# Attention heads issued as steps between weight stages, and another way to transpose queries, in a four-layer decoder trunk

## The chip, the cores and the metric

The kernel runs on one core of one Trainium2 chip. The metric is the device time of one execution in microseconds. Before the change three runs gave 2584.72, 2582.40 and 2582.67 us: a median of 2582.67.

## What is computed

A trunk of four layers on 256 tokens of width 2048, in float32. Each layer normalizes its input and multiplies it by one input matrix. That gives the streams of a token mixer, four query heads for attention over a memory of 256 tokens, and a gate. The heads' outputs are multiplied by SiLU(gate), go through an output matrix and are added to the residual. The mixers are, in order, latent attention (layer 0), sparse attention with an indexer (layer 1), sliding-window attention with a learned sink for each head (layer 2), and latent attention again (layer 3). A last normalization follows.

The change concerns layers 1 and 2. Both have 32 query heads of 64 features, in four groups of eight that share a key and a value head, and both add a bias by relative position. Of the reference (layer 2; layer 1 has no sink, and masks what the indexer did not select):

```python
s = jnp.einsum('bqgjd,bkgd->bgjqk', qb, kb, preferred_element_type=jnp.float32) * scale + bias
s = jnp.where(valid, s, NEG_INF)
m = jnp.maximum(jnp.max(s, axis=-1, keepdims=True), sink)
e = jnp.exp(s - m)
p = e / (jnp.sum(e, axis=-1, keepdims=True) + jnp.exp(sink - m))
return jnp.einsum('bgjqk,bkgd->bqgjd', p.astype(vb.dtype), vb)
```

## The kernel before

**Matrix products.** TensorE's products of two float32 matrices are made of three: each operand is a high part (the value rounded to the float32r type) and a low part (what is left), and high by high, high by low and low by high are summed. Weights come from HBM in stages of 2 or 4 tiles of 128 rows (`stage`, L206), loaded by SyncE's queue into five buffers. `parts_of` (L234) cuts a tile into its parts: ScalarE rounds it (through `copy_act`, L60), VectorE subtracts (in `split`, L69). There are three buffers of each part. `rows_by` (L240) gives tokens by columns, with the matmuls of L265 to L267; `columns_by` (L270) gives features by tokens, with those of L285 and L289. Both add up in a pair of the four PSUM tiles called acc.

**Steps.** `steps` (L227) is a list of Python generators. At each stage `other_work` (L229) advances the first of them twice, so that its instructions come into the program between two stages' matmuls. In layer 1 the indexer's selection is such a generator; in layer 3 a split of weights for the end is one. A row product over 2048 features has 8 stages, a gate has 8 (two products of 4), an output projection has 8 (four column chunks of 2), and the memory part's two query products have 8 together.

**Layers.** A layer runs six parts in the order memory heads 0 and 1 (part 4), groups 0 to 3, memory heads 2 and 3 (part 5). For each part it issues the projection, then the attention, and then `w_out` (L1134), the output projection of the part *before*. That adds into the residual x at L1139.

**A group** (class Grouped). `project` (L913) makes the eight heads' queries with `rows_by`, transposes them and makes the gate (`gate`, L474). In layer 1 `four_heads` (L461) takes the unsplit rows, transposes 4 blocks for each half of the heads (L467) and splits while it copies out of PSUM (L60, L471). In layer 2 `stacked` (L795) splits the rows first (L60, L801), sets the high and the low part of a head beside each other and transposes 16 blocks in float32r (`transposed`, L449, matmuls at L456). Then GpSimd's queue loads the group's table of biases, bm (L930), 1 MB, into a tile with one buffer, so the load waits until the group before has read its own.

`attend` (L934) first empties `steps`, and then issues all eight heads. A head is two score products (L943, L946), a bias and a running maximum on VectorE (L520 to L522), exponentials on ScalarE (L527), sums and reciprocals, three transposes of the weights (L502), and another split (L60, L69). After each second head comes the product with the values for both (L972). Heads 0 to 3 and 4 to 7 fill one half of y each, by a product with the gate (L978) and a split.

**Order.** `TileContext` sorts each engine's instructions itself, by what it takes to be ready at which time. What stands earlier in the program goes first among what is ready. So the trace's order isn't the program's, and waits are added where buffers or data are shared.

**Memory heads.** `memory_project` (L551) loads stored keys and values through GpSimd's queue and makes queries and a gate; `memory_attend` (L569) has two heads, with L580 as their score matmul and L601 as that with the values.

Of the kernel before, what the change touches and what calls it, by code (L numbers as in the profile page):

```python
# [8 lines left out]
F32 = mybir.dt.float32  # L9
# [6 lines left out]
P = 128  # L16
S = 256
# [9 lines left out]
N_TAB = 384  # L27
# [4 lines left out]
def kernel(ctx: ExitStack, tc: tile.TileContext, a: dict, out: bass.AP,  # L32
                             kinds=(0, 1, 2, 0)):
    nc = tc.nc
# [3 lines left out]
    act = ctx.enter_context(tc.tile_pool(name="act", bufs=1))  # L38
# [14 lines left out]
    def f32(ap):  # L53
        return ap.bitcast(F32)

    def part_tile(dt=F32R):
        return wk.tile([P, 512], dt, name="hl", tag="hl", bufs=2)

    def copy_act(o, i, scale=1.0):
        inst = nc.scalar.activation(o, i, AF.Copy, scale=scale)  # L60
        if pinned:
            tc.keep_in_program_order(inst)
# [164 lines left out]
    steps = []  # L227

    def other_work():  # L229
        for _ in range(2):  # L230
            if steps and next(steps[0], None) is None:
                steps.pop(0)

    def parts_of(wr, c0, n):  # L234
        wh = wp.tile([P, 512], F32R, name="wh", tag="wh", bufs=3)
# [225 lines left out]
    def four_heads(dst, rows_):  # L461

        tp = misc("tr")
        for t in range(2):
            for p in range(2):
                c = (2 * p + t) * P
                nc.tensor.transpose(tp[:, c:c + P], rows_[t][:, p * P:(p + 1) * P], ident)  # L467
        for h, main, low in ((0, slice(0, 64), slice(64, P)), (1, slice(64, P), slice(0, 64))):
            feats = tp[main].rearrange("p (j c) -> p j c", j=2)
            copy_act(dst[main, h::2, :], feats)  # L470
            nc.vector.tensor_sub(dst[low, h::2, :], feats, f32(dst)[main, h::2, :])  # L471


    def gate(nm, w, c0):  # L474
        gT = act.tile([P, 4, S], F32, name="gT", tag="gT", bufs=2)
        for h in range(2):
            acc = columns_by(nm.at, 16, w, 0, (c0 + h * S, S), "g")
            for j in range(2):
                z = total(acc[j])
                hz = wk.tile([P, S], F32, name="hz", tag="z", bufs=3)  # L480
                nc.vector.tensor_mul(hz, z, nm.half)
                th = wk.tile([P, S], F32, name="th", tag="e", bufs=4)
                nc.scalar.activation(th, hz, AF.Tanh)
                nc.vector.scalar_tensor_tensor(gT[:, 2 * h + j, :], th, 1.0, hz, op0=OP.add, op1=OP.mult)
        return gT
# [261 lines left out]
    class Grouped:  # L747
# [165 lines left out]
        def project(self, g):  # L913
            nm = self.nm
            acc = rows_by(nm.at, 16, self.w, 0, (g * 512, 512), "q")
            q = [act.tile([P, 4, S], F32R, name="qS", tag="pq", bufs=PQ) for z in range(2)]
            if self.sparse:
                for z in range(2):
                    rows_ = part_tile(F32)
                    for t in range(2):  # L920
                        copy_act(rows_[:, t * S:(t + 1) * S], acc[t][:, z * S:(z + 1) * S],
                                 scale=nm.col("eighth", t))
                    four_heads(q[z], [rows_[:, t * S:(t + 1) * S] for t in range(2)])
            else:
                for t in range(2):
                    self.stacked(lambda i0, i1: q[i0 // 4][:, :, t * P:(t + 1) * P], acc[t],
                                 nm.col("eighth", t), 8)
            bm = act.tile([P, 8, S], F32, name="bm", tag="big3")
            tab = tabs[0 if self.sparse else 1][g]
            nc.gpsimd.dma_start(bm, bass.AP(tensor=tab.tensor, offset=tab.offset + 127,  # L930
                                            ap=[[8 * N_TAB - 1, P], [N_TAB, 8], [1, S]]))
            return g, q, bm, gate(nm, self.w, self.g0 + g * 512)

        def attend(self, g, q, bm, gT):  # L934
            while steps:
                other_work()
            y = act.tile([P, 2, 4, S], F32R, name="y", tag="y", bufs=2)
            for h in (0, 2, 1, 3, 4, 6, 5, 7):
                def score(b):
                    sp = misc("sp")  # L940
                    qb = q[h // 4][:, h % 4, b * P:(b + 1) * P]
                    if b == 0:
                        nc.tensor.matmul(sp[:, :S], qb, self.k[:, g, :, :P], start=True, stop=True)  # L943
                    else:
                        for v in range(2):
                            nc.tensor.matmul(sp[:, :S], qb, self.k[:, g, v, :],  # L946
                                             start=v == 0, stop=v == 1)
                    return sp

                def bias(b, n):  # L950
                    bh = bm[:, h, S - n:]
                    if not self.sparse:
                        return bh
                    bs = wk.tile([P, S], F32, name="bs", tag="e", bufs=4)
                    nc.vector.tensor_add(bs[:, :n], bh, self.sel[:, b, :n])
                    return bs[:, :n]
                nsk = None if self.sparse else nsink[:, g * 8 + h:g * 8 + h + 1]
                tp = masked_softmax(score, bias, None, nsk)

                half, odd = h // 2 % 2, h % 2  # L960
                if half == 0:
                    pHL = [wk.tile([P, 3, 2, P], F32R, name="pT2", tag="pT", bufs=PT) for z in range(2)]
                split(pHL[0][:, :, half, :], pHL[1][:, :, half, :],
                      tp[:, :3 * P].rearrange("p (i c) -> p i c", i=3))
                if half == 0:
                    continue
                if not odd:
                    o = misc("o")
                v0 = g * P + (0 if odd else 64)
                for t in range(2):  # L970
                    for n_, (z, p_) in enumerate(((0, 0), (0, 1), (1, 0))):
                        nc.tensor.matmul(o[:, t * S:], self.vz[z][:, t, v0:v0 + P],  # L972
                                         pHL[p_][:, 2 * t:2 + t].rearrange("p i h c -> p (i h c)"),
                                         start=odd == t == n_ == 0, stop=odd == t == 1 and n_ == 2)
                if odd:
                    j = (h // 4) * 2
                    yt = tmp("yt")
                    nc.vector.tensor_mul(yt.rearrange("p (j b c) -> p j b c", j=2, b=2),  # L978
                                         o.rearrange("p (b j c) -> p j b c", b=2, j=2),
                                         gT[:, j:j + 2, :].rearrange("p j (b c) -> p j b c", b=2))  # L980
                    split(y[:, 0, j:j + 2, :], y[:, 1, j:j + 2, :], yt.rearrange("p (a b) -> p a b", a=2))
            return y


    def last_out(w, part, y):
# [140 lines left out]
    for i in range(depth):  # L1126
        kind = kinds[i]
        mixer = Latent(nm, i, kinds[:i].count(0)) if kind == 0 else Grouped(nm, i, kind == 1)
        mixer.first()
        if i == depth - 1:  # L1130
            steps.append(split_ahead(a["w_out"][i], 5))
        nxt = Norm(i + 1) if i + 1 < depth else None

        def w_out(part, y, last):  # L1134
            for c in range(4):
                acc = rows_by([y], 4, a["w_out"][i], part * 4, (c * 512, 512), "wo")
                for t in range(2):
                    xs = x[t][:, c * 512:(c + 1) * 512]
                    nc.vector.tensor_add(xs, xs, acc[t])  # L1139
                if c == 0 and copies:  # L1140

                    not_before(xs[:, :1])
                    table_copies(*copies.pop(0))
                if last and nxt is not None:
                    nxt.chunk(c)

        pending = None
        order = [4, 0, 1, 2, 3, 5]
        for n_, part in enumerate(order):
            if part >= 4:  # L1150
                y = memory_attend(*memory_project(nm, i, mixer.w, mixer.mq0, mixer.g0, part - 4,
                                                  f32(mixer.k[:, 0] if kind else mixer.kr)[:, 0, :1]))
            else:
                y = mixer.attend(*mixer.project(part))
            if pending is not None:
                w_out(*pending, False)
            pending = (part, y)
        if nxt is None:
            last_out(a["w_out"][i], *pending)
        else:  # L1160
            w_out(*pending, True)
            nxt.finish()
            nm = nxt
# [62 lines left out]
```

## Time and profile before

| | |
|---|---|
| median of three runs | 2582.67 us |
| the profiled execution, whole | 2583.45 us |
| its span, from the first to the last instruction | 2581.7 us |
| granted TensorE clock, mean | 0.999 |
| TensorE weight loads busy | 2210.8 us |
| VectorE, ScalarE busy | 1885.5, 1618.6 us |
| DMA | 520.02 MB, 201 GB/s in the mean |

Layer 1 runs from about 959 us of the span to 1492, layer 2 from there to about 1975. In the profile PE is TensorE's matmuls, PEld its weight loads, DVE VectorE, ACT ScalarE, POOL GpSimd, SP SyncE. L467 is line 467 of the kernel; a helper's line stands for all its callers, so the tiles' names (out<-in) tell which it was. In rows in order of time, the first number is the start in us from the span's beginning and the second the length. Matmuls overlap in their pipeline, so the time that one costs is the distance to the start of the next. "[0.34 <-DVE ms L583]" is idle time before an instruction, and what ended it. In rows of stretches each engine has its busy time and the number of its instructions, in the order PE, PEld, DVE, ACT, POOL, then the granted clock, the share of the DMA engines, and GB/s.

### The profile page before, as it was taken

The page shows a single profiled execution, that of the slowest core. Times are in us where ns is not written, and L with a number is a line of the kernel's source. Part 1 is how long each engine was busy: PE and PEld are TensorE (multiplying, and loading weights), DVE is VectorE, ACT ScalarE, POOL GpSimd, SP SyncE. Part 2 cuts the span into 40 slices and gives each one's busy share as a digit, 9 for nine tenths or more (in the row PEclk, how much of TensorE's full clock was granted, in tenths as well). Part 3 has the DMA queues.
Part 4 walks back from the last instruction along what each step waited for, and adds up shares of the span by engine and source line. Part 5 has one row for each costly group of instructions (what it writes and reads, how often), then busy time and mean ns, then how long its engine had stood idle before and what let it go on. Part 6 is the DMA issues. An engine that isn't in the chain of part 4 may idle for free. (4 is left out here: it accounts for less than half of the span.)

```text
span 2581.7 us, 41595 instructions
## 1 busy us (share of the span) xinstructions
PE 2569.7 (100%) x13986; PEld 2210.8 (86%) x13986; DVE 1885.5 (73%) x4139; ACT 1618.6 (63%) x3435; POOL 87.1 (3%) x159
## 2 busy tenths in 40 slices
PE   9999999999999999999999999999999999999998
PEld 7888898888888888888888888888888888888887
DVE  6666667677776686877778776777778767777676
ACT  6556556556656566667666666676666655665655
POOL 1000000000000010000000000000000000000000
PEclk9999999999999999999999999999999999999999
DMA  9888777666676667566556565555555877666664
GB/s 301 257 258 268 239 213 235 183 172 192 192 205 200 199 213 248 169 203 188 190 171 197 171 221 170 173 174 185 196 156 147 241 201 197 196 195 182 211 173 179
DMA packets 459416, 520.02 MB, mean 201 GB/s; under 512 B 69520, under 2 KB 353056, under 8 KB 457536
## 3 DMA queue, kind: packets, MB, share of 16 engines
q1 hardware_dynamic: 441744, 449.72, 58.1%
q0 software_dynamic: 16736, 66.65, 8.0%
q8 instruction: 110, 1.80, 0.3%
q14 instruction: 106, 0.87, 0.1%
q10 hardware_dynamic: 720, 0.98, 0.1%
HBM read 494.10 MB, written 35.75 MB: 205 GB/s over the span
## 5 line engine op out<-in xcount | busy, mean ns | idle before, releaser
L69 DVE TENSOR_TENSOR wl<-wr,wh 128x512 fp32r<-128x512 f32 (+2 forms) x1720 | 1159.9, 677 | 610.0 <-ACT wh L60 588.8
L60 ACT ACTIVATE wh<-wr 128x512 fp32r<-128x512 f32 (+2 forms) x1720 | 1065.3, 621 | 796.6 <-PE acc_g L285 176.9
L285 PE MATMUL acc_g<-xT,wh 128*128 128x512 f32 x1536 | 486.0, 396 | 0.0
L289 PEld LDWEIGHTS acc_g<-xT,wl 128*128 128x128 f32 x1536 | 284.6, 188 | 61.7
L289 PE MATMUL acc_g<-xT,wl 128*128 128x256 f32 x1536 | 307.9, 280 | 0.0
L266 PE MATMUL acc_wo<-wl,y 128*128 128x512 f32 x752 | 297.1, 395 | 0.2 <-DVE wl L69 0.2
L267 PE MATMUL acc_wo<-wh,y 128*128 128x512 f32 x752 | 292.0, 390 | 0.0
L285 PEld LDWEIGHTS acc_g<-xT,wh 128*128 128x128 f32 x1536 | 237.1, 189 | 2.7
L265 PE MATMUL acc_wo<-wh,y 128*128 128x512 f32 x752 | 234.5, 392 | 0.1
L266 PEld LDWEIGHTS acc_wo<-wl,y 128*128 128x128 f32 x752 | 141.3, 188 | 27.9 <-DVE wl L69 0.6
L267 PEld LDWEIGHTS acc_wo<-wh,y 128*128 128x128 f32 x752 | 141.3, 188 | 27.1
L265 PEld LDWEIGHTS acc_wo<-wh,y 128*128 128x128 f32 x752 | 139.1, 188 | 28.7 <-ACT y L60 1.0
L285 PE MATMUL acc_mq<-xT,wh 128*128 128x512 f32 x512 | 161.6, 396 | 0.0
L285 PE MATMUL acc_mk<-mT,wh 128*128 128x512 f32 x512 | 161.5, 396 | 0.1
L1139 DVE TENSOR_TENSOR x<-x,acc_wo 128x512 f32<-128x512 f32 x184 | 121.4, 681 | 3.7 <-PE acc_wo L267 3.6
L285 PE MATMUL acc_qn<-cT,wh 128*128 128x512 f32 x384 | 121.3, 397 | 0.0
L285 PE MATMUL acc_cq<-xT,wh 128*128 128x512 f32 x384 | 120.9, 396 | 0.0
L289 PEld LDWEIGHTS acc_mk<-mT,wl 128*128 128x128 f32 x512 | 96.1, 188 | 22.8 <-DVE wl L69 0.4
L289 PEld LDWEIGHTS acc_mq<-xT,wl 128*128 128x128 f32 x512 | 93.9, 188 | 20.1
L289 PE MATMUL acc_mq<-xT,wl 128*128 128x256 f32 x512 | 103.1, 281 | 0.0
L266 PE MATMUL acc_q<-wl,xT 128*128 128x512 f32 x256 | 101.2, 395 | 0.0
L289 PE MATMUL acc_mk<-mT,wl 128*128 128x256 f32 x512 | 101.1, 278 | 0.0
(328 smaller groups left out, 4326.2 us busy)
## 6 DMA issues: line engine op xcount, KB each, us to landing
wr<-in_w_out_dram SPq DMA_DIRECT2D x188, 512.0 KB, 3.7
wr<-in_w_in_a_dram SPq DMA_DIRECT2D x176, 512.0 KB, 4.5
wr<-in_w_mem_kv_dram SPq DMA_DIRECT2D x120, 512.0 KB, 4.6
wr<-in_w_in_b_dram SPq DMA_DIRECT2D x112, 512.0 KB, 3.4
wr<-in_w_in_c_dram SPq DMA_DIRECT2D x104, 512.0 KB, 3.5
wr<-in_w_uq_dram SPq DMA_DIRECT2D x192, 128.0 KB, 2.9
wr<-in_w_uq_dram SPq DMA_DIRECT2D x48, 256.0 KB, 3.8
tab<-flat POOLq DMA_DIRECT2D x8, 1536.0 KB, 9.7
```

The source lines that it names most:

```text
L60: inst = nc.scalar.activation(o, i, AF.Copy, scale=scale)
L69: nc.vector.tensor_sub(lo, src, f32(hi))
L265: nc.tensor.matmul(acc[t][:, :n], xh, wh[:, :n], start=first, stop=False)
L266: nc.tensor.matmul(acc[t][:, :n], xh, wl[:, :n], start=False, stop=False)
L267: nc.tensor.matmul(acc[t][:, :n], xl, wh[:, :n], start=False, stop=last)
L285: nc.tensor.matmul(acc[j], wh[:, o:o + P], q[:, :, kt % 4, :], start=kt == 0, stop=False)
L289: nc.tensor.matmul(acc[j][:, 0, :], wl[:, o:o + P], q[:, 0, kt % 4, :], start=False, stop=kt == kts - 1)
L1139: nc.vector.tensor_add(xs, xs, acc[t])
```

## The change

- `attend` of a group no longer issues its eight heads. It puts them as a generator (`heads`) into `steps`, in the order 0, 2, 1, 3, 4, 6, 5, 7, with 0, 6, 6, 5, 4, 4, 5 and 7 yields ahead of them. They come into the program between the stages of what follows: the output projection of the part before, the next queries, the next gate (or the memory part's products).
- Layer 2 transposes its queries as layer 1 does.
- The biases' tile is made once for a layer. Each group loads it in two halves, the first (heads 0 to 3) in `project`, the second in `attend`, after the steps are emptied.
- Ahead of the memory heads 2 and 3 of layers 1 and 2, `steps` is emptied.

```diff
+    def finish_steps():
+        while steps:
+            other_work()
...
             q = [act.tile([P, 4, S], F32R, name="qS", tag="pq", bufs=PQ) for z in range(2)]
-            if self.sparse:
-                for z in range(2):
-                    rows_ = part_tile(F32)
-                    for t in range(2):
-                        copy_act(rows_[:, t * S:(t + 1) * S], acc[t][:, z * S:(z + 1) * S],
-                                 scale=nm.col("eighth", t))
-                    four_heads(q[z], [rows_[:, t * S:(t + 1) * S] for t in range(2)])
-            else:
+            for z in range(2):
+                rows_ = part_tile(F32)
                 for t in range(2):
-                    self.stacked(lambda i0, i1: q[i0 // 4][:, :, t * P:(t + 1) * P], acc[t],
-                                 nm.col("eighth", t), 8)
-            bm = act.tile([P, 8, S], F32, name="bm", tag="big3")
+                    copy_act(rows_[:, t * S:(t + 1) * S], acc[t][:, z * S:(z + 1) * S],
+                             scale=nm.col("eighth", t))
+                four_heads(q[z], [rows_[:, t * S:(t + 1) * S] for t in range(2)])
+            if g == 0:
+                self.bm = act.tile([P, 8, S], F32, name="bm", tag="big3")
+            self.load_bias(g, 0)
+            return g, q, self.bm, gate(nm, self.w, self.g0 + g * 512)
+
+        def load_bias(self, g, half):
+
             tab = tabs[0 if self.sparse else 1][g]
-            nc.gpsimd.dma_start(bm, bass.AP(tensor=tab.tensor, offset=tab.offset + 127,
-                                            ap=[[8 * N_TAB - 1, P], [N_TAB, 8], [1, S]]))
-            return g, q, bm, gate(nm, self.w, self.g0 + g * 512)
+            nc.gpsimd.dma_start(self.bm[:, 4 * half:4 * half + 4, :],
+                                bass.AP(tensor=tab.tensor, offset=tab.offset + 127 + 4 * half * N_TAB,
+                                        ap=[[8 * N_TAB - 1, P], [N_TAB, 4], [1, S]]))
 
         def attend(self, g, q, bm, gT):
-            while steps:
-                other_work()
+
+            finish_steps()
+            self.load_bias(g, 1)
             y = act.tile([P, 2, 4, S], F32R, name="y", tag="y", bufs=2)
-            for h in (0, 2, 1, 3, 4, 6, 5, 7):
+            steps.append(self.heads(y, g, q, bm, gT))
+            return y
+
+        def heads(self, y, g, q, bm, gT):
+            for h, ahead in ((0, 0), (2, 6), (1, 6), (3, 5), (4, 4), (6, 4), (5, 5), (7, 7)):
+                for _ in range(ahead):
+                    yield True
                 def score(b):
...
             if part >= 4:
-                y = memory_attend(*memory_project(nm, i, mixer.w, mixer.mq0, mixer.g0, part - 4,
-                                                  f32(mixer.k[:, 0] if kind else mixer.kr)[:, 0, :1]))
+                projected = memory_project(nm, i, mixer.w, mixer.mq0, mixer.g0, part - 4,
+                                           f32(mixer.k[:, 0] if kind else mixer.kr)[:, 0, :1])
+                if kind and part == 5:
+                    finish_steps()
+                y = memory_attend(*projected)
```

More of the change, by code (lines that the diff above doesn't have):

```diff
@@ L981, in attend @@
                     split(y[:, 0, j:j + 2, :], y[:, 1, j:j + 2, :], yt.rearrange("p (a b) -> p a b", a=2))
-            return y
     def last_out(w, part, y):
```

## Prediction

> **What bounds the kernel now.** I read the page first, then busy time by stretches, then TensorE's instructions in order of time. From the page:
>
> ```profile
> span 2581.7 us, 41595 instructions
> ...
> PE 2569.7 (100%) x13986; PEld 2210.8 (86%) x13986; DVE 1885.5 (73%) x4139; ACT 1618.6 (63%) x3435; POOL 87.1 (3%) x159
> ...
> L69 DVE TENSOR_TENSOR wl<-wr,wh 128x512 fp32r<-128x512 f32 (+2 forms) x1720 | 1159.9, 677 | 610.0 <-ACT wh L60 588.8
> L60 ACT ACTIVATE wh<-wr 128x512 fp32r<-128x512 f32 (+2 forms) x1720 | 1065.3, 621 | 796.6 <-PE acc_g L285 176.9
> ```
>
> TensorE is busy for 2569.7 of 2581.7 us, so 12.0 us at most is plain idleness. The engines that cut each weight tile into two parts (L60, then L69) have room: ScalarE's largest wait before L60 is for matmuls. TensorE is what they wait for, not the other way round. One group of the layer with sinks (eight heads, the next queries, a gate, an output projection) looks like this in the view of stretches:
>
> ```profile
> 1717.40:1794.80 77.40, 77.40 (x409) 65.57 (x409) 59.32 (x149) 53.00 (x130) 0.89 (x1) 1.00 0.57 177
> ```
>
> In 77.4 us TensorE is never idle, while VectorE is free for 77.4 - 59.3 = 18.1 us and ScalarE for 24.4. The change touches just these stretches: four groups in layer 1 and four in layer 2. So only two things can shorten them: fewer cycles of TensorE's own, and the few places at which a matmul starts late.
>
> Are the heads in one lump now, because the code issues all eight ahead of the output projection? The row for the first score matmul of a head, over the window 1636 to 1700, says no:
>
> ```profile
> L943 PE MATMUL sp<-kd,qS x7: 280/363/364, 1639.1 to 1695.2; 128*128 128x256 f32 x7
> ```
>
> Seven starts lie over 56.1 us, one head every 9.4 us, in a period of 77.4. The order that is made out of the program has spread them already.
>
> **The change, term by term.**
>
> Term 1, the transposes of the queries in layer 2. Now a group splits its queries into high and low halves first, and transposes 16 blocks. TensorE's rows in order of time (start, length, instruction):
>
> ```profile
> 1689.97 0.88 PE L456 MATMUL tr<-identr,hl 128*128 128x128 f32 x8
> 1690.69 0.46 PE L266 MATMUL acc_wo<-wl,y 128*128 128x512 f32 x1
> 1690.99 0.39 PE L267 MATMUL acc_wo<-wh,y 128*128 128x512 f32 x1
> ...
> 1693.73 0.46 PE L456 MATMUL tr<-identr,hl 128*128 128x128 f32 x4
> 1694.02 1.05 PE L972 MATMUL o<-pT,vz 128*128 128x512 f32 x5
> 1694.91 0.46 PE L456 MATMUL tr<-identr,hl 128*128 128x128 f32 x4
> 1695.20 0.35 PE L943 MATMUL sp<-kd,qS 128*128 128x256 f32 x1
> ```
>
> Lengths overlap, so I take starts. The eight occupy 1690.69 - 1689.97 = 0.72 us, the fours 0.29 each, 1.30 in all. The instruction behind a run holds TensorE longer as well: the L266 at 1690.69 takes 0.30 to the next start, against the 0.22 of the same matmul from 1929.52 to 1929.74 below. That is some 0.07 for each of three runs. Sum: 1.30 + 0.21 = 1.51 us a group.
>
> After the change layer 2 does what layer 1 does: transpose the unsplit queries, 8 blocks. Layer 1 shows the price:
>
> ```profile
> 1203.35 1.04 PE L467 MATMUL tr<-ident,hl 128*128 128x128 f32 x8
> 1204.14 0.48 PE L289 MATMUL acc_g<-xT,wl 128*128 128x256 f32 x2
> 1204.46 0.39 PE L285 MATMUL acc_g<-xT,wh 128*128 128x512 f32 x1
> ...
> 1205.14 0.40 PE L289 MATMUL acc_g<-xT,wl 128*128 128x256 f32 x2
> 1205.38 0.63 PE L285 MATMUL acc_g<-xT,wh 128*128 128x512 f32 x2
> ```
>
> 0.79 us for the eight, and the pair behind them takes 0.32 instead of 0.24: 0.87 us. The saving is 1.51 - 0.87 = 0.64 a group, 4 x 0.64 = 2.6 us. A transpose costs 0.09 us here (the fours, 0.36 with the tail) to 0.11 (the eight of layer 1), so the ends are 4 x (16 x 0.09 - 8 x 0.11) = 2.2 and 4 x (16 x 0.10 - 8 x 0.10) = 3.2 us. I take 2.6, the one read from whole groups.
>
> The Trainium skill, "TensorE: Matmul & The Clock Gate", section "LDWEIGHTS (loading the stationary operand)", has a weight load take its columns divided by 1.2 ns, 107 for 128; by that price alone the term would be 4 x 8 x 0.107 = 3.4 us. Layer 1's transposes agree with it (0.87 / 8 = 0.109), layer 2's are cheaper (0.094), and the rows decide.
>
> The other engines pay for this in VectorE's time: four splits of one kind go, four of another come, from the rows by tile.
>
> ```profile
> L801 DVE SCALAR_TENSOR_TENSOR hl<-acc_q,x,hl x16: 475/478/485, 1592.2 to 1844.6; 128x256 fp32r<-128x256 f32 x16
> ```
>
> ```profile
> L471 DVE TENSOR_TENSOR qS<-tr,qS x16: 674/684/696, 1112.4 to 1361.3; 64x512 fp32r<-64x512 f32 x16
> ```
>
> 4 x (0.684 - 0.478) = 0.8 us a group, inside VectorE's 18.1 us of free time: nothing, or 4 x 0.8 = 3.3 us if that cover were gone. ScalarE does four copies before and four after the transposes either way.
>
> Term 2, the end of each layer. The last group's y is wanted while the memory heads run. Layer 2, then layer 1:
>
> ```profile
> 1926.94 0.39 PE L972 MATMUL o<-pT,vz 128*128 128x512 f32 x1
> 1927.67 1.09 PE L972 MATMUL o<-pT,vz 128*128 128x512 f32 x5 [0.34 <-DVE ms L583]
> ...
> 1929.52 0.39 PE L266 MATMUL acc_wo<-wl,y 128*128 128x512 f32 x1
> 1929.74 0.39 PE L267 MATMUL acc_wo<-wh,y 128*128 128x512 f32 x1
> 1930.21 0.50 PE L265 MATMUL acc_wo<-wh,y 128*128 128x512 f32 x1
> ```
>
> ```profile
> 1443.29 0.64 PE L265 MATMUL acc_wo<-wh,y 128*128 128x512 f32 x2
> 1444.08 0.50 PE L266 MATMUL acc_wo<-wl,y 128*128 128x512 f32 x1 [0.15 <-DVE wl L69]
> ...
> 1444.88 0.40 PE L267 MATMUL acc_wo<-wh,y 128*128 128x512 f32 x1
> 1445.34 0.50 PE L265 MATMUL acc_wo<-wh,y 128*128 128x512 f32 x1
> ```
>
> Against 0.23 a matmul these lose 0.50, 0.24, 0.33 and 0.23: 1.3 us. The last head's probabilities and the memory heads' softmax stand in the same two queues at once. The new code finishes the last group's heads inside the gate of the memory part (step 38 of 48, counted below), so they end first. I take the whole 1.3, with ends 0 and 1.3.
>
> Term 3, the spacing itself. Heads now come as steps behind the weight splits of their stage, no longer ahead of all of them. Nothing in the middle of a group is late now, so nothing is gained. What may be lost is the slow rival's price; I take 0. Regrouped transposes of the heads (3 x 64, at 0.09 to 0.11 each) could shift 192 x 0.01 = 1.9 us either way; I take 0.
>
> Term 4, the bias tables. One load a group becomes two halves, on GpSimd's queue:
>
> ```profile
> 1685.63 0.91 POOL L930 DMA_DIRECT2D bm<-tab  x1 [155.18 <-DVE mn L522]
> ...
> bm<-tab POOLq DMA_DIRECT2D x8, 1024.0 KB, 7.5
> ```
>
> The load waits for the last head's read, starts at 1685.63 and lands 7.5 us later at 1693.1, 2.1 us ahead of the first score at 1695.20. The first half now waits only for heads 0 to 3 and lands sooner; the second is wanted from the fifth head on. Behind them in that queue stand the memory part's loads, as before. GpSimd works 0.89 us in a group, and eight more issues of 0.91 hide there: 0.
>
> Sum: -2.6 - 1.3 = -3.9 us. The profiled execution took 2583.45 us (its span and 1.75 around it), so 2579.6 for it; it lies 0.8 above the median of 2582.67, which gives **2578.8 us**, 0.15% faster.
>
> **The rivals.**
>
> A, the steps order nothing new. The heads are spread already, so the order that is made may come out as before, ends of the layers included. Only term 1 is left: 2582.7 - 2.6 = 2580.1. For it: the 9.4 us between heads now. Against: the last group's heads really are issued earlier relative to the memory heads.
>
> B, slower: the last head of a group comes too late for the output projection that needs its y. The waits between yields add up to 37, so this head is the 38th step; a stage takes two, and the output projection and the queries have eight stages each, so step 38 falls in the third of the gate's eight. A gate without anything between:
>
> ```profile
> 1541.99:1564.28 22.29, 22.29 (x128) 19.41 (x128) 0.83 (x2) 0.73 (x2) 1.00 0.61 191
> ```
>
> Six of eight stages are 16.7 us of cover, and twelve first matmuls of the projection (2.7) need only the other half of y. This head's chain now:
>
> ```profile
> 1682.54 0.36 PE L943 MATMUL sp<-kd,qS 128*128 128x256 f32 x1
> ```
>
> From there to the end of its output (1694.02 + 1.05) are 12.5 us, and 1.3 more for product and split, at the splits' 0.68 and 0.62. So 19.4 - 13.8 = 5.6 us are to spare. The chain crosses engines some 12 times; if each crossing stands behind one more split of 0.65, it grows by 7.8 us, and 2.2 are lost in each of eight groups: 17.6 us, 2596. It decides from about nine splits more in the chain. Against it: VectorE's 18 us and ScalarE's 24 free in a group.
>
> C, faster by over 0.2%: all of terms 1 and 2, and the heads' transposes fall well (-1.9): 2582.7 - 5.8 = 2576.9. The Trainium skill, "Perfetto Trace Analysis", section "Identifying the Most-Contended Engine", would have TensorE's room judged by its weight loads and not its busy time; those are at 86% here, and if the rest were room, this rival would be likelier. The starts speak against it: 0.22 to 0.23 us a matmul wherever nothing is named as late.
>
> **How the numbers follow.** Forecast (terms 1 and 2) 0.44, A 0.21, B 0.20, C 0.15. About 0.2% (5.2 us) is what a measurement of this kernel tells from no change: faster is C, 0.15; within it are the forecast and A, 0.65; slower is B, 0.20. The range leaves most of B out: from 2576.0, with C and term 1 at its upper end, to 2586.0, where term 2 stays, VectorE's cover fails (3.3) and the regrouping falls badly (1.9), with a little of B.
>
> **What would show it.** Term 1: in layer 2 the transposes come as eight L467-like rows a group and 16 L456-like rows go; a middle group takes 76.8 us for 77.4. Term 2: no gap over 0.1 us at the o matmuls and the first acc_wo of the two layers' ends. Term 4: bias loads that wait for less than a period and no VectorE wait for them. Wrong would be a wait of acc_wo for y in each group (B), a group that keeps 77.4 us, or any shift outside layers 1 and 2.

## The result, and the profile after

The changed kernel takes **2598.01 us** (median of six runs, 2597.55 to 2599.56), against 2582.64 for the kernel before in the runs beside it: a ratio of 1.0059, with a 95% interval from 1.0046 to 1.0072. It is 15.4 us slower. The forecast was 2578.8, and the range ended at 2586.0.

The page of the changed kernel, the lines that answer to those shown for the kernel before (busy time; mean of one in ns; then idle time of the engine in front of it and what ended most of it):

```profile
span 2597.8 us, 41552 instructions
...
PE 2576.4 (99%) x13954; PEld 2210.4 (85%) x13954; DVE 1892.3 (73%) x4139; ACT 1620.8 (62%) x3435; POOL 91.7 (4%) x167
...
L69 DVE TENSOR_TENSOR wl<-wr,wh 128x512 fp32r<-128x512 f32 (+2 forms) x1720 | 1160.1, 677 | 622.1 <-ACT wh L60 599.2
L60 ACT ACTIVATE wh<-wr 128x512 fp32r<-128x512 f32 (+2 forms) x1720 | 1064.6, 621 | 804.6 <-PE acc_g L289 173.0
...
L269 PE MATMUL acc_wo<-wh,y 128*128 128x512 f32 x752 | 238.2, 396 | 9.8 <-ACT wh L60 5.2
```

The last of them before:

```profile
L265 PE MATMUL acc_wo<-wh,y 128*128 128x512 f32 x752 | 234.5, 392 | 0.1
```

The work of the other engines is nearly as before (VectorE has 6.8 us more). TensorE has 32 instructions fewer (eight in each of four groups) and yet a longer span. What has changed is the first product of an output projection, L269 (L265 before): TensorE is idle for 9.8 us in front of it, where it was 0.1. Line numbers from L234 to L917 are 4 higher than before.

Where the time went shows in the view of stretches, with a layer cut at the first matmul of its own key and value product and at that of the next layer. Before, layers 1 and 2 (length, then busy time of PE, PEld, DVE, ACT and POOL with their instructions, granted clock, DMA share, GB/s):

```profile
959.09:1492.10 533.01, 532.79 (x2898) 456.88 (x2896) 423.41 (x985) 358.97 (x808) 17.43 (x26) 1.00 0.61 191
1492.10:1975.54 483.44, 482.78 (x2591) 410.76 (x2590) 361.74 (x836) 316.78 (x726) 7.18 (x12) 1.00 0.57 179
```

After:

```profile
958.76:1498.69 539.93, 536.10 (x2897) 455.96 (x2896) 425.17 (x985) 359.07 (x808) 20.23 (x31) 1.00 0.61 189
1498.69:1991.75 493.06, 485.92 (x2560) 411.21 (x2558) 366.60 (x836) 318.72 (x726) 8.97 (x15) 0.99 0.57 175
```

Layer 1 is 6.9 us longer and layer 2 9.6: 16.5 of the 16.1 us by which the spans differ. The rest of the program is as before to 0.4 us. From the starts of all matmuls I also add up how much later than 0.23 us (for 512 columns, in proportion for fewer) the next one starts, where that is over 0.1 us (in layer 1 without the indexer's transposes). These "late starts" rise from 0.97 to 7.47 us in layer 1 and from 1.46 to about 10.1 in layer 2. Another 3.2 us there are matmuls at half rate, of which more at the end; the shorter transposes take 2.2 off. Together that is layer 2's 9.6.

The view of waits names what TensorE's weight loads wait for (total us, times, longest). Before:

```profile
PEld acc_wo L265 <- ACT wh L60: 0.3, 1, 0.3
PEld acc_wo L265 <- ACT y L60: 1.0, 2, 0.5
```

After:

```profile
PEld acc_wo L269 <- ACT wh L60: 8.7, 10, 1.2
PEld acc_wo L269 <- ACT y L60: 3.8, 6, 1.3
```

The output projection waits for y, the outputs of the last two heads. The waits put down to wh, which are the larger part, I read as the same thing: the weights' high parts have three buffers, and while matmuls with y can't run, none comes free for the next. For this reading speaks that in the group below the late starts of the projection begin behind its twelfth matmul, at 1698.66, and twelve are those that need only the first half of y. Two more waits, 2.3 us of the 9.8, end with a z of the gate on VectorE. TensorE's rows in order of time, in one group of layer 2 of the changed kernel:

```profile
1690.85 0.27 PE L506 MATMUL ptp<-ident,e 128*128 128x128 f32 x1
1690.96 1.04 PE L471 MATMUL tr<-ident,hl 128*128 128x128 f32 x8
1691.83 0.38 PE L506 MATMUL ptp<-ident,e 128*128 128x128 f32 x2
...
1696.23 0.28 PE L955 MATMUL sp<-kd,qS 128*128 128x256 f32 x1
...
1703.22 0.27 PE L506 MATMUL ptp<-ident,e 128*128 128x128 f32 x1
...
1705.86 1.21 PE L984 MATMUL o<-pT,vz 128*128 128x512 f32 x6
...
1709.65 0.50 PE L269 MATMUL acc_wo<-wh,y 128*128 128x512 f32 x1 [1.10 <-ACT y L60]
```

The three ptp from 1690.85 on transpose the weights of the last head but one, the sp at 1696.23 is the last head's score. Between them stand the next queries' eight transposes. In the kernel before, the last head's score came at 1682.54, and the queries' transposes from 1689.97 on, so behind it. There the score stood right behind the first of these ptp (1682.52 and 1682.54); here it is 5.4 us behind, its product with the values ends at 1707, and the projection waits until 1709.65.

Layer 1 shows the same. Before:

```profile
1195.12 0.27 PE L502 MATMUL ptp<-ident,e 128*128 128x128 f32 x1
1195.14 0.36 PE L943 MATMUL sp<-kd,qS 128*128 128x256 f32 x1
...
1203.24 0.27 PE L502 MATMUL ptp<-ident,e 128*128 128x128 f32 x1
1203.35 1.04 PE L467 MATMUL tr<-ident,hl 128*128 128x128 f32 x8
```

After:

```profile
1194.79 0.27 PE L506 MATMUL ptp<-ident,e 128*128 128x128 f32 x1
1194.90 0.82 PE L471 MATMUL tr<-ident,hl 128*128 128x128 f32 x6
...
1200.18 0.28 PE L955 MATMUL sp<-kd,qS 128*128 128x256 f32 x1
...
1208.21 0.27 PE L506 MATMUL ptp<-ident,e 128*128 128x128 f32 x1
```

The score is 5.0 us later. TensorE is not idle in those 5 us: the gate's matmuls fill them. So it isn't a wait at that place but the order that was made. The stall comes 12 us later, at the projection.

### The profile page after: what moved, and what is told of

It reads as the page before. It is cut to its first block, busy times and chain, and to the rows that moved or that the text cites. A ratio compares the mean times of both kernels' runs of the same rounds, so it can differ in the third digit from the quotient of the medians.

```text
span 2597.8 us, 41552 instructions
## 1 busy us (share of the span) xinstructions
PE 2576.4 (99%) x13954; PEld 2210.4 (85%) x13954; DVE 1892.3 (73%) x4139; ACT 1620.8 (62%) x3435; POOL 91.7 (4%) x167
## 5 line engine op out<-in xcount | busy, mean ns | idle before, releaser
L289 PE MATMUL acc_g<-xT,wh 128*128 128x512 f32 x1536 | 484.2, 396 | 0.0
L269 PE MATMUL acc_wo<-wh,y 128*128 128x512 f32 x752 | 238.2, 396 | 9.8 <-ACT wh L60 5.2
L269 PEld LDWEIGHTS acc_wo<-wh,y 128*128 128x128 f32 x752 | 138.2, 189 | 41.5 <-ACT wh L60 8.7
```

The lines of the kernel that those rows point to most:

```text
L269: nc.tensor.matmul(acc[t][:, :n], xh, wh[:, :n], start=first, stop=False)
L289: nc.tensor.matmul(acc[j], wh[:, o:o + P], q[:, :, kt % 4, :], start=kt == 0, stop=False)
```

## The experiments

**Theory T**: the last head is behind the next queries' transposes in the program now (its 37 yields end in the gate; the transposes stand ahead of the gate), so they go first, and the head's output is late. Rivals: S, the spacing of the heads costs by itself; B (not the prediction's rival B), the bias tables' halves cost; and the new transposes of layer 2 could cost by themselves. Each run stands beside runs of the kernel before on the same chip (2582.6 to 2582.8); the ratio to these has a 95% interval behind it.

### The two edits, apart

**e1_transposes_only**: the kernel before, with the new transposes in layer 2.

```diff
-            if self.sparse:
                 for z in range(2):
                     rows_ = part_tile(F32)
...
                     four_heads(q[z], [rows_[:, t * S:(t + 1) * S] for t in range(2)])
-            else:
-                for t in range(2):
-                    self.stacked(...)
```

> The kernel before, with layer 2's queries transposed unsplit (8 transposes a group for 16) and nothing else changed. All theories: only the first term of the sum is tested here. If it was sized right, 2582.6 - 2.6 = 2580.0 us, between 2579.4 and 2580.4. If the new way of transposing is itself what costs, over 2585.

Measured: 2587.36 us (2586.78 to 2588.74), 1.0018 [1.0008, 1.0027]. The new transposes, which were to save 2.6 us, cost 4.7.

**e2_heads_ahead**: the changed kernel; the heads are finished ahead of the next queries' transposes.

```diff
+            if g:
+                finish_steps()
             q = [act.tile([P, 4, S], F32R, name="qS", tag="pq", bufs=PQ) for z in range(2)]
```

> The changed kernel, but in groups 1 to 3 the steps are emptied just ahead of the next queries' transposes, so that only the last head changes its place: it comes ahead of them. Theory T (the transposes take two of the four PSUM buffers that a head's scores need, so the last head starts some 8 us later and the output projection waits for its y): the late starts of the middle groups go, 2578 to 2581 us. Theory S (spacing as such: heads stand behind the weight splits): seven of eight heads stay spaced, so most of the loss stays, over 2592. Theory B (the biases in halves through GpSimd's queue come late): near 2598.

Measured: 2588.05 us, 1.0020 [1.0011, 1.0030]. Ten microseconds are gone, all that the change has beyond e1. It lies between the forecasts: theory T's, 2578 to 2581, left out that e1's loss would stay.

**e3_heads_at_once**: the changed kernel; all heads are issued right where `attend` did it before.

```diff
             steps.append(self.heads(y, g, q, bm, gT))
+            finish_steps()
```

> The changed kernel, but the steps are emptied as soon as a group's heads have been put into them: all eight heads ahead of the output projection, as before the change; the biases still come in halves. T and S: both causes are gone, 2578 to 2582 us. B: the halves are still there, near 2598.

Measured: 2588.23 us, 1.0023 [1.0014, 1.0032]: as e2, so the spacing up to the transposes neither gains nor costs. Both forecasts missed, for the same reason as in e2.

**e4_last_behind**: the changed kernel; seven heads at once, and only the last at its step.

```diff
-((0, 0), (2, 6), (1, 6), (3, 5), (4, 4), (6, 4), (5, 5), (7, 7))
+((0, 0), (2, 0), (1, 0), (3, 0), (4, 0), (6, 0), (5, 0), (7, 37))
```

> The changed kernel with no waits ahead of the first seven heads (all seven at once, ahead of the output projection) and 37 ahead of the last: this one stays in the gate, behind the next queries' transposes. T: the last head still stands behind the transposes, so the loss stays, 2592 to 2602 us. S: seven heads are no longer spaced, most of the loss goes, 2579 to 2586. B: near 2598.

Measured: 2598.55 us, 1.0060 [1.0043, 1.0076]: the whole loss. One head's place against the transposes is enough.

**f3_spaced_old_transposes**: the changed kernel with layer 2's transposes of before.

> The changed kernel with layer 2's old way of transposing (split first, 16 blocks). T, that transposes ahead of the last head cost by the buffers they hold: layer 1 keeps its 6.9 us; in layer 2 the old transposes hold a buffer for one copy, so little is lost there: 2588 to 2592. If the two losses simply add: 2598.0 less 4.7 for the new transposes, 2593.3.

Measured: 2599.07 us, 1.0062 [1.0047, 1.0077]. Both forecasts missed: with the old transposes nothing of the loss goes.

**f5_ahead_old_transposes**: e2 with layer 2's transposes of before.

> The changed kernel with the heads finished ahead of the next queries' transposes, and with layer 2's transposes of before: only the spacing up to there, the halves of the bias tables and the end of the two layers are left of the change. If the two edits tested so far (last head behind the transposes, new transposes in layer 2) hold the whole loss: 2581 to 2583, within 1.5 us of before, with no late start at layer 2's end. If the spacing or the halves cost something that the other runs hid: 2584 or more.

Measured: 2582.66 us, 1.0001 [0.9991, 1.0010]. Its layers in the view of stretches:

```profile
958.76:1491.77 533.01, 532.79 (x2898) 456.92 (x2897) 423.57 (x985) 358.97 (x808) 20.58 (x31) 1.00 0.62 191
1491.77:1974.71 482.94, 482.54 (x2591) 410.83 (x2590) 361.77 (x836) 316.73 (x726) 8.98 (x15) 1.00 0.57 179
```

Layer 1 is what it was before to 0.01 us and layer 2 is 0.5 shorter. Spaced heads and halved tables are free (S and B fall), and the two edits together hold the whole loss:

| | old transposes in layer 2 | new ones |
|---|---|---|
| all heads ahead of the transposes | 2582.64 (before), 2582.66 (f5) | 2587.36, 2588.05, 2588.23 (e1, e2, e3) |
| the last head behind them | 2599.07 (f3) | 2598.01 (after), 2598.55 (e4) |

The two don't add: once the last head is behind, it makes no difference which transposes it is behind.

### Why is the last head late behind the transposes?

Heads and transposes share four PSUM tiles, for scores, weights, outputs and transposed queries. **Theory H**: a transposes' tile is held too long, until its copies and subtractions are done. **Theory V**: it is the burst of subtractions on VectorE. If H holds, emptying the tiles early with one copy must help.

**f1_early_release**: e1, with layer 2's tile emptied first. **f4_changed_early_release**: the same in the changed kernel, in both layers.

```diff
+            held = tp
+            tp = tmp("trs")
+            copy_act(tp, held)
```

> The kernel before with the new transposes in layer 2, whose PSUM buffer ScalarE now empties with one copy; the split is made from that copy, with the same four subtractions on VectorE. That run without the copy had late starts of 8.5 us in layer 2 and 2587.4 us. Theory H (the transposes hold their PSUM buffers through four instructions each, where the old ones held them for one copy): the late starts go, 2580 to 2582 us. Theory V (four subtractions of 0.68 us come in one burst on VectorE just as the last head's weights and y pass there): nothing changes for VectorE, and ScalarE has two copies more, 2587 to 2590.

Measured: 2592.07 us, 1.0036 [1.0023, 1.0049], slower than e1 by 4.7 and above both forecasts. The early release also gives ScalarE two copies more in each group.

> The changed kernel with the transposes' PSUM buffers emptied by one copy in layers 1 and 2, all else as it is. T in its form that buffers held are what delays the last head: layer 1 loses most of its 6.9 us and layer 2 some, 2585 to 2590. In its form that the transposes' work on ScalarE and VectorE, not their buffers, goes ahead of the last head: no gain, 2596 to 2602.

Measured: 2601.36 us, 1.0071 [1.0054, 1.0088]. In the group of layer 1 shown above, the tiles were empty by 1197.5 and the last head's score came at 1199.70, against 1200.18. So how long a tile is held explains little: layer 1 is 1.4 us shorter than in the changed kernel (538.52 us), layer 2 is 3.4 longer (496.48). How much of a gain the two extra copies a group hide was not tested.

**f2_pool_minus**: f1, with layer 2's subtractions on GpSimd in place of VectorE.

> The same as the early release, with the four subtractions of a group on GpSimd in place of VectorE. H: as the early release, 2580 to 2582. V: the late starts of layer 2 go here and not there, 2579 to 2583 here, if GpSimd is no slower than some 3 us for one.

Measured: 2594.02 us, 1.0042 [1.0027, 1.0057]. Both forecasts missed, and it doesn't test V: a subtraction takes 1.45 us there, and scores wait for it (4.0 us in layer 2).

```profile
L476 POOL TENSOR_TENSOR qS<-trs,qS x16: 1262/1451/1724, 1596.0 to 1863.4; 64x512 fp32r<-64x512 f32 x16
```

**g2_last_later**: the changed kernel with the last head 7 steps later, `(7, 14)` for `(7, 7)`.

> The changed kernel with the last head 7 steps later (the 45th step in place of the 38th, so 3.5 stages of the gate, about 9.8 us of program). If the place in the program decides how late the last head is (theory T, and the price of the slow rival): each of up to eight groups loses some microseconds more, 2605 to 2660. If the made order takes the last head at the first chance wherever it stands behind the transposes, as the run with all heads together up to the last let it seem: 2597 to 2600.

Measured: 2594.75 us, 1.0049 [1.0034, 1.0063], faster than the changed kernel. Both forecasts missed. The number of steps does not set the price; why this place is 3 us better was not settled.

**g4_transposes_behind_gate**: the changed kernel; queries are copied out as before, but transposed only behind the gate, so that all heads are ahead of them.

```diff
+            gT = gate(nm, self.w, self.g0 + g * 512)
+            for z in range(2):
+                four_heads(q[z], [held[z][:, t * S:(t + 1) * S] for t in range(2)])
```

> The changed kernel with one move: the next queries are copied out of PSUM as before, but transposed and split only behind the gate's two products, so that every head, the last too, stands ahead of them in the program. If the order of the last head and the transposes is the cause of both losses (theory T, and the loss of the new transposes by themselves): no wait of the output projection for y is left, the saving on TensorE and the layers' ends show, 2577 to 2581. If the transposes and their splits delay whatever chain runs beside them, wherever they stand: the first head of the next group is late now, or something else, 2586 to 2600.

Measured: 2587.80 us, 1.0022 [1.0012, 1.0031]. T's loss is gone a third way. What stays is e1's, which the first forecast had going too: the made order is nearly e1's again (layer 2 is 488.51 us, in e1 488.66).

### Why do the new transposes cost by themselves?

In e1 the last head is in its old place, yet layer 2 is 5.2 us longer, with 8.5 us of late starts instead of 1.5. One group of e1, VectorE in order of time:

```profile
1693.04 0.68 DVE L69 TENSOR_TENSOR wl<-wr,wh 128x512 fp32r<-128x512 f32 x1
1693.76 1.28 DVE L471 TENSOR_TENSOR qS<-tr,qS 64x512 fp32r<-64x512 f32 x2
1695.07 0.56 DVE L69 TENSOR_TENSOR pT<-ptp,pT 128x384 fp32r<-128x384 f32 x1
...
1697.43 0.69 DVE L471 TENSOR_TENSOR qS<-tr,qS 64x512 fp32r<-64x512 f32 x1
1698.16 0.69 DVE L973 TENSOR_TENSOR yt<-o,gT 128x512 f32<-128x512 f32 x1
```

TensorE:

```profile
1691.57 0.27 PE L502 MATMUL ptp<-ident,e 128*128 128x128 f32 x1
1691.68 1.03 PE L467 MATMUL tr<-ident,hl 128*128 128x128 f32 x8
...
1695.68 1.09 PE L967 MATMUL o<-pT,vz 128*128 128x512 f32 x5 [0.46 <-DVE pT L69]
...
1699.91 0.51 PE L265 MATMUL acc_wo<-wh,y 128*128 128x512 f32 x1 [1.24 <-ACT y L60]
```

The eight transposes stand between the last head's own (ptp). With them four subtractions fall due on VectorE, and they take turns with that head's weights (pT) and its product with the gate (yt). Before, VectorE's part for the queries (the hl of L801, 0.48 us each) came ahead of the transposes that read it: in this group two of the four some 25 us earlier (1665.47 and 1667.47), and two beside the last head (1691.74 and 1693.55). ScalarE had four copies out of the transposes' tiles then too. Two runs take the work behind the transposes away; what they leave out stands in their expectations.

**g1_no_low_parts**: e1 without layer 2's subtractions. **h1_no_parts**: without ScalarE's copies too.

```diff
-            copy_act(dst[main, h::2, :], feats)
-            nc.vector.tensor_sub(dst[low, h::2, :], feats, f32(dst)[main, h::2, :])
+            nc.gpsimd.memset(f32(dst)[main, h::2, :], 0.0)
+            nc.gpsimd.memset(f32(dst)[low, h::2, :], 0.0)
```

> The kernel before with the new transposes in layer 2, but with the low parts of layer 2's queries left out (set to zero by GpSimd): four subtractions of 0.68 us a group less on VectorE, everything else as in the run of the new transposes alone (2587.4). If VectorE's subtractions are what delays the last head's output (theory V): the late starts of layer 2 fall from 8.5 us to below 2, the saving on TensorE remains, 2579 to 2582. If the place of the transposes and the copies on ScalarE do it: still 2586 to 2588. A time between says how much is VectorE's.

Measured: 2585.03 us, 1.0009 [1.0000, 1.0019]. Layer 2:

```profile
1491.18:1976.42 485.24, 482.54 (x2560) 408.43 (x2558) 354.57 (x820) 318.32 (x726) 15.46 (x28) 1.00 0.57 178
```

> As the run without the low parts, but the high parts of layer 2's queries are left out too (both zeroed by GpSimd; the transposes still run): neither ScalarE nor VectorE has work behind the transposes. If the burst of copies on ScalarE and subtractions on VectorE behind the transposes is the whole of what the new transposes cost (theory V, widened to both engines): the late starts of layer 2 fall from 5.3 us without the low parts to 1 to 2, 2579 to 2581.5. If the transposes delay the last head by their place alone: no further gain, 2584 to 2586.

Measured: 2581.76 us, 0.9997 [0.9988, 1.0007]. Layer 2:

```profile
1491.34:1973.47 482.13, 481.62 (x2559) 408.53 (x2558) 356.24 (x820) 309.66 (x710) 23.29 (x44) 1.00 0.57 179
```

Layer 2 goes from 488.7 us by 485.2 to 482.1, and its late starts from 8.5 by 5.3 to 2.3. Without VectorE's 16 subtractions 3.4 us come back, without ScalarE's 16 copies too another 3.1 (2.3 and 3.3 by the medians; g1 lies between its two forecasts, h1 0.3 us above the lower one). So the loss goes with the work behind the transposes, and the subtractions, for which the prediction's sum had put nothing, are about half of it. The other half is not shown to be ScalarE's. The kernel before has 16 such copies as well, of 0.60 us, and loses nothing by them, so h1 leaves out work that was always there. That they cost now because they come closer together (four from 1692.72 to 1696.35 in e1, from 1690.55 to 1696.00 before) is argued. And in h1 nothing reads the transposes' tiles, so these come free at once too; f1, where they came free early, speaks against that as the cause, though with two copies more in each group.

### Tiles of another kind

The queries lie ready some 26 us ahead of their transposes (in e1 they are copied out at 1663.6 to 1665.9 and transposed at 1691.7). If the shared tiles tie transposes and heads together, a tile out of the projections' four (acc) must set them free.

**h2_changed_acc**: the changed kernel. **h3_transposes_acc**: e1.

```diff
-        tp = misc("tr")
+        tp = ps.tile([P, 512], F32, name="tr", tag="acc", bufs=4)
```

> The changed kernel, with the transposed queries of layers 1 and 2 put into one of the four PSUM tiles of the projections (acc), not into one of the four that scores, weights and outputs of the heads share. The rows are copied out 28 us before they are transposed, so with a buffer of their own kind the transposes can come at once, far ahead of the last head. If it is the shared buffers that put transposes and last head side by side: both losses go, only the saving on TensorE and the layers' ends are left, 2578 to 2581, faster than before. If the made order sets them side by side for another reason: 2590 to 2600. If the projections now wait for a tile: new late starts at the first matmuls of a gate, 2585 to 2600.

> The kernel before with the new transposes in layer 2, and with the transposed queries of both layers put into a PSUM tile of the projections (acc). If the shared buffers put the transposes beside the last head: the late starts of layer 2 fall from 8.5 us to below 2.5, 2579 to 2582. If not: 2586 to 2589. If the projections wait for a tile instead: late starts at a gate's first matmuls, 2585 to 2595.

Measured: 2613.64 us, 1.0123 [1.0108, 1.0138], and 2612.93, 1.0117 [1.0100, 1.0134]. Both forecasts of the whole missed, by an oversight: layers 0 and 3 use the helper too and lose 12 us each, where transposes now stand close behind VectorE's rotation of their queries (qrr). The waits of h2:

```profile
PEld tr L471 <- DVE qrr L618: 18.0, 12, 2.2
PEld tr L471 <- ACT hl L60: 4.7, 14, 0.9
```

But layer 2 has 484.2 and 484.1 us, and layer 1 537.6 in both. **i1_own_tiles** leaves layers 0 and 3 alone; **i2_own_tiles_between** also transposes only between the gate's two products.

> The changed kernel with the transposed queries in a PSUM tile of the projections, now in layers 1 and 2 alone (the last two runs did it in layers 0 and 3 as well, which share the helper, and these lost 12 us each). If the two layers keep the lengths that they had there (537.6 and 484.2 us): 2587 to 2588.5, so nearly all of layer 2's loss is gone though the heads are still spaced as in the change. If the gain there hung on the other layers: 2595 or more.

Measured: 2589.12 us, 1.0024 [1.0014, 1.0033], 0.6 above the first forecast; the two layers keep their lengths to 0.6 us (537.51 and 484.73).

> As the other, but the queries are transposed between the two products of the gate, 11 us behind their copy out of PSUM, so that no transpose waits for the copy. If these waits (4.7 us in the last run but one) are what is left: both layers come to or below the kernel before, 2578 to 2582. If the gate's second product waits for the tiles instead: late starts at its first matmuls, 2584 to 2600.

Measured: 2586.79 us, 1.0015 [1.0006, 1.0025]. The time lies in the second forecast's range, but no matmul of the gate starts late, so neither forecast holds. Layer 2 of i1, and its last head in the group looked at above:

```profile
1496.30:1981.03 484.73, 483.44 (x2559) 408.17 (x2558) 366.00 (x836) 317.52 (x726) 8.98 (x15) 1.00 0.57 178
```

```profile
1686.71 0.27 PE L506 MATMUL ptp<-ident,e 128*128 128x128 f32 x1
1686.74 0.36 PE L955 MATMUL sp<-kd,qS 128*128 128x256 f32 x1
```

The score follows its ptp at once again, though the head is as far behind the transposes in the program as in the changed kernel; the transposes come at 1669.4. Of layer 2's 9.6 us, 8.3 are gone. So in layer 2 it is the shared tiles that make the last head late: with other tiles for the transposes, and nothing else changed, it isn't. By what way they do it is not shown. That the sorting hands out such tiles in the program's order, and so can't let the head past, is the reading that fits f4 and i1 both; it was not tested by itself. In i1 the transposes and the work behind them also come some 20 us earlier, away from the last head, and this run can't tell the two apart. Layer 1 keeps 3.4 to 4.5 us of its loss, some of it transposes waiting for their copy (2.7 us in i1, none in i2). What is left in i2 stands at the projection again (waits of 1.7 us for y, 1.7 for wl, 1.2 for wh), and its cause is open. No version that computes the queries beat the kernel before: f5 equals it.

## Why the prediction was wrong

Two steps failed, and the larger is in term 3: what the last head's place costs was put at nothing, and it alone costs 16.4 us (f3 against f5). The other is in term 1: the cover for the new transposes' work, 4.7 us alone (e1). Together they are 15.4, so they don't add. The sign that the prediction had named for being wrong, a wait of acc_wo for y, is there, but not in each group.

- **The bound** was right: TensorE is 99% busy, and only its own cycles and late starts count. All loss is late starts and their half rate.
- **Term 1** (2.6 saved, ends 2.2 and 3.2): the saving is there and at its lower end. Without late starts layer 2 takes 483.44 - 1.46 = 481.98 before and 482.13 - 2.33 = 479.80 in h1: 2.2 us. **The step that failed here is the cover**, "inside VectorE's 18.1 us of free time: nothing". It set 0.8 us of extra time against the free time of a whole group. What counted was when the work comes: 4 x 0.68 us on VectorE in the few microseconds in which the last head's weights, product and split pass through it (2.3 to 3.4 us by g1). The rest goes with ScalarE's copies in h1; why they cost more than before is open. Net of the saving the edit cost 4.7 us; the alternative that was priced, 3.3 us, was of the right kind and too small.
- **Term 2** (1.3): 0.5. In f5 layer 2 gained it; in layer 1, 533.01 us stayed 533.01.
- **Term 3** (0): right for the spacing as such (f5, e3), **wrong for the last head**. Its yields carry it past the transposes of the next queries, and that was not looked at: the step counted stages from step 38 and the chain's 13.8 us, and took it that the head starts when its step is reached. It starts behind what the program has put ahead of it in the same tiles, 5 us later in the groups shown of both layers.
- **Term 4** (0): right. The loads are halved and nothing of TensorE waits for them.
- **Rival B** (0.20; 2596) named the place, the output projection that waits for y, and nearly the time, 2598. Its mechanism was another: one more split at each of 12 crossings. What happened is one shift of 5 us at one place, which all but uses up the 5.6 us of cover that it had worked out; that the burst behind the transposes does the rest is argued, not shown. That the price agreed is chance. Nor is the loss spread over eight groups. In layer 1 three groups have some 2 us of late starts each. In layer 2 the loss lies in two, the one shown and the one at about 1860, with some 7 and 6 us, half rate included; the group at about 1777 has none.

## What to carry to other kernels

Price an added operation where it will stand: by the free time of its engine in the few microseconds in front of the wait that ends last there, not by its free time in a period. When work is moved later in a program, list what it is moved past that takes buffers from the same small set; with such a set the order of the program bound here even where all engines had room. And before counting on slack at a deadline, find the first instruction of the chain in the new order, not in the old.

## What the runs showed of the hardware

**The granted clock halved after short pauses in quick succession**, twice in layer 2. The changed kernel, behind the wait of 1.10 us that ended at 1709.65, in stretches:

```profile
1706.50:1709.60 3.10, 1.48 (x10) 0.99 (x9) 2.64 (x9) 2.50 (x9) 0.00 (x0) 1.00 0.40 148
1709.60:1713.50 3.90, 3.85 (x11) 3.03 (x12) 1.54 (x7) 1.98 (x7) 0.00 (x0) 0.61 0.00 0
```

TensorE was busy for 1.48 of 3.10 us, and then ran for 3.4 us at half rate: starts from 1710.46 to 1713.45 are 0.43 us apart instead of 0.23. The same happened from 1864.02 on, again for 3.4 us. In the 3.4 us ahead of the two falls TensorE was busy for 1.74 and 1.75. Each stretch cost 1.6 us, though no single pause was longer than 1.2 us. But not every such stretch was followed by a fall: from 1699.06 to 1702.47 TensorE was busy for 1.25 of 3.41 us, and the clock stayed. What decides is not shown. The Trainium skill, "TensorE: Matmul & The Clock Gate", "Part 1: The HAM clock gate", has the clock at half after an idle window of about 3.4 us and at full after as long a busy one. The length of the slow stretch agrees; the fall came after a stretch of 3.1 us in which TensorE was half busy, not idle.

**GpSimd took twice VectorE's time for the same subtraction**: 1.45 us for 64x512 (f2) against 0.69 (f1).
